# Attention rows of an output projection: split fp32 parts or native fp32 on TensorE

## The chip, the cores and the metric

The kernel runs on one core of one Trainium2 chip. The metric is the device time of one execution in microseconds (us). TensorE (PE, with its weight loads as PEld), VectorE (DVE), ScalarE (ACT), GpSimd (POOL) and SyncE (SP, which here only issues DMAs) run beside each other and meet at semaphores.

## The reference

Two layers, 256 positions (two row tiles of 128), width 1024, fp32 throughout. What matters here is the mixer and the projection that ends it:

```python
for i in range(DEPTH):
    h = h + 0.5 * _swiglu_ffn(_rms_norm(h, ffn1_norm[i]), ffn1_w_gate_up[i], ffn1_w_down[i])
    u = _rms_norm(h, mix_norm[i])
    q, k, v, ca, cg = jnp.split(u @ w_in[i], SPLITS, axis=-1)
    ...
    attn = _sliding_window_attention(q, k, v, sinks[i])
    conv = _conformer_conv(ca, cg, conv_w[i], conv_b[i], conv_ln_g[i], conv_ln_b[i])
    mixed = jnp.concatenate([_rms_norm(attn, attn_out_norm[i]),
                             _rms_norm(conv, conv_out_norm[i])], axis=-1)
    h = h + mixed @ w_out[i]
    h = h + 0.5 * _swiglu_ffn(_rms_norm(h, ffn2_norm[i]), ffn2_w_gate_up[i], ffn2_w_down[i])
    e = _rms_norm(p[i] @ w_ple[i], ple_norm[i])
    h = h + jax.nn.sigmoid(h @ w_ple_gate[i]) * e
```

`attn` and `conv` are 512 wide each, so `w_out` has 512 attention rows and 512 convolution rows.

## The kernel before

Every large product is made of reduced fp32 parts. A weight tile `raw` comes by DMA, ACT casts it to `hi` (type fp32r), DVE or POOL subtracts to get `lo`, and `triple` (line 201) makes three matmuls of it: high by high, high by low, low by high (128 rows by 128 columns held, 512 columns streamed). A few products stay in plain fp32 instead: the scores (`kT`, `qT`), probabilities times values (`pT`, `v`), and the per-layer embedding (`pinT` by `raw32`, the tile name of a unit built without an engine). The profile records each plain fp32 matmul as two weight loads and two matmuls.

Weights go through rings of tiles: 4 slots for `raw`, 10 for `hi` and 10 for `lo`, taken in program order; a new tile waits until the one ten before it is done with.

A mixer runs as follows. Convolution inputs (`c0`, `c1`, channels split in halves), keys and values, then queries are projected; DVE applies the rotary embedding (lines 786 to 789); the depthwise convolution's 31 taps run in the background, on DVE (line 565) and as ACT products that POOL adds (lines 553, 557); the result of a half is `y` (line 567). Scores of the two row blocks follow (`sm`, line 630), then values (`v0`, `v1`), and `attn_out` (line 672): the product `o` with the reciprocal denominators, times the gain on POOL into `a`, and `a` split into `a_split` (a high part by ACT, line 689, and a low part by DVE). `uwa` are the two weight units of the attention rows, 512 columns each, of four chunks; `uwc` are those of the convolution rows.

The tail follows the string `TAIL`, "a00 s0 s1 a01 t0 a10 t1 a11 b0 b1": `a<t><n>` multiplies the attention of row tile t by column half n (`out_rows`, line 718), `s` and `t` are the layer norm of the convolution (transposes of `y` and of `yn`), `b` the convolution rows. PE's order there is fixed by the program (`manual_schedule`). The other engines' order, and PE's elsewhere, come from a scheduler that plays the program through with its own costs, so leaving instructions out also reorders others.

Of the kernel before, what the change touches and what calls it, by code (L numbers as in the profile page):

```python
# [11 lines left out]
F32 = mybir.dt.float32  # L12
F32R = mybir.dt.float32r
# [6 lines left out]
P = 128  # L20
# [51 lines left out]
UWAP = (1, 3)  # L72
# [3 lines left out]
def hybrid_trunk_kernel(  # L76
# [28 lines left out]
    V, S, GP, T = nc.vector, nc.scalar, nc.gpsimd, nc.tensor  # L105
# [3 lines left out]
    wk = ctx.enter_context(tc.tile_pool(name="wk", bufs=2))  # L109
# [9 lines left out]
    def tbank():  # L119
        return pt.tile([P, 512], F32, tag="tp", name="tbank")  # L120

    def wf(name="wf"):
        return wk.tile([P, 512], F32, tag="wf", name=name, bufs=NWF)
# [7 lines left out]
    def split_lo(eng, lo, src, hi):  # L131
        return eng.tensor_tensor(out=lo, in0=src, in1=hi.bitcast(F32), op=ALU.subtract)  # L132
# [2 lines left out]
        def __init__(self, enter, first, rest):  # L135
            self.enter, self.first, self.rest = enter, first, rest

    # ---------------------------------------------------------------- weights
    pool_lo = []

    class Unit:
# [51 lines left out]
    def unit_attn_rows(w, c0, cn, eng=V):  # L193
        def half(kv):
            def part(raw, k0, ku):
                src = w[kv * G * HD:(kv + 1) * G * HD, c0:c0 + cn].rearrange("(g d) n -> d g n", d=HD)
                return raw[kv * HD:(kv + 1) * HD], src[:, k0:k0 + ku, :]
            return part
        return Unit(G, cn, [half(0), half(1)], eng)

    def triple(xh, xl, wh, wl):
        return [(xh, wh), (xh, wl), (xl, wh)]
# [15 lines left out]
    def ordered():  # L218
        return tc.manual_schedule(engines=MANUAL)

    # -------------------------------------------------------------- constants
    h = [cp.tile([P, D], F32, name=f"h{t}") for t in range(2)]

    def h_load(t):
# [20 lines left out]
    def gain(l, name):  # L245
        o, n = off[name]
        return pcol[:, o + l * n:o + (l + 1) * n]
# [21 lines left out]
        T.transpose(tb[:, 0:NPR], prow, ident[0:NPR, 0:NPR])  # L269
        V.tensor_copy(pcol[:, 16:16 + NPR], tb[:, 0:NPR])  # L270

    # -------------------------------------------------- norms and transposes
    def scratch():
        return wk.tile([P, D], BF16, tag="wf", name="scratch", bufs=NWF)

# [19 lines left out]
    def bc(g, n=P):  # L295
        return g.unsqueeze(2).to_broadcast([P, g.shape[1], n])
# [22 lines left out]
    def transposed(X, t, b, g):  # L319
        x_split(X, t, b, x_gather(X, t, b, g))  # L320

    # -------------------------------------------------------------------- ffn
    def ffn_stage(l, wgu, wdn, gname, side, early):
        X, r = [None, None], [None, None]
        H1, HT, DN, GU, acc = {}, {}, {}, {}, []
# [85 lines left out]

        return Stage(enter, first, rest)

    # ------------------------------------------------------------------- rope
    cos2 = [cp.tile([P, 16], F32, name=f"cos{t}") for t in range(2)]
    sin2 = [cp.tile([P, 16], F32, name=f"sin{t}") for t in range(2)]

# [66 lines left out]
        V.tensor_scalar(out=ms, in0=tb[:, 0:1], scalar1=1.0 / n, scalar2=None, op0=ALU.mult)  # L484
        return rms_r(ms)

    # ------------------------------------------------------------------ mixer
    def mixer_stage(l, PT, EMB):
        w = w_in[l]
        X, r, r8 = [None] * 2, [None] * 2, [None] * 2  # L490
# [27 lines left out]
    def mixer(l, w, X, r, r8, CI, CV, proj, conv_load, PT, EMB, nxt):  # L518
# [1 line left out]
        E, emb = ple(l, up, PT)  # L520
        EMB.extend(E)

        # ---- convolution inputs and depthwise convolution
        cb = gain(l, "cb")
        Y = []

# [40 lines left out]
                V.tensor_tensor(out=y, in0=acc, in1=yp, op=ALU.add)  # L567
            Y.append(y)

        # ---- q, k, v  # L570
        ukv = unit_plain(w, 0, 8, 512, 256)
        uq = unit_plain(w, 0, 8, 0, 512)
        qT = [None, None]
# [29 lines left out]
                qT[t] = wf("qT")  # L603
                S.copy(qT[t], tb)

        # ---- attention
        DEN = [None]
        AS = []
        AT, rA, PR, RX, OB = ([None] * 2 for _ in range(5))
# [62 lines left out]
        def attn_out(b):  # L672
            ob, rexp = OB[b], RX[b]
            tb = tbank()
            for gg in range(G):
                T.transpose(tb[:, gg * P:(gg + 1) * P], rexp[:, gg * P:(gg + 1) * P], ident)
            rT = wf("rT")
            S.copy(rT, tb)
            o = wf("o")
            V.tensor_tensor(out=o, in0=ob, in1=rT, op=ALU.mult)  # L680
            sq = wf("sq")
            S.activation(sq, o, AF.Square)
            a = wf("a")
            GP.tensor_tensor(out=a.rearrange("q (k m) -> q k m", k=4), in0=o.rearrange("q (k m) -> q k m", k=4),
                             in1=bc(gain(l, "attn")), op=ALU.mult)
            if b == 0:
                AS.append(wk.tile([P, 4, 512], F32R, tag="pr", name="a_split", bufs=1))
            hi, lo = AS[0][:, 2 * b, :], AS[0][:, 2 * b + 1, :]
            S.copy(hi, a)
            split_lo(V, lo, a, hi)  # L690
            AT[b] = (hi, lo)
            rA[b] = feature_r(sq, CH)

        for it in ORDER.split():
# [16 lines left out]
            elif it[0] == "o":  # L711
                attn_out(int(it[1]))

        uwa = [unit_attn_rows(w_out[l], n * 512, 512, V) for n in range(2)]
        for u in uwa:
            u.load({}, UWAP)

        def out_rows(us, F, t, rr, n, hooks=()):
            b = bank()
            terms = []  # L720
            for k in range(4):
                cs = slice(k * P, (k + 1) * P)
                terms += triple(F[0][:, cs], F[1][:, cs], us[n].hi(k), us[n].lo(k))
            mms(b, terms, hooks=hooks)
            ns = slice(n * 512, (n + 1) * 512)
            V.scalar_tensor_tensor(out=h[t][:, ns], in0=b, scalar=rr, in1=h[t][:, ns],
                                   op0=ALU.mult, op1=ALU.add)
# [60 lines left out]
        V.tensor_tensor(out=t2[:, :, 8:16], in0=q[:, :, 0:8], in1=s3[:, :, 8:16].to_broadcast([P, n, 8]), op=ALU.mult)  # L788
        V.tensor_tensor(out=q[:, :, 0:16], in0=t1, in1=t2, op=ALU.add)

    # -------------------------------------------------------------------- ple
    def bcast_row(ap, n, tag="wf", bufs=NWF):
        b = wk.tile([P, 512], F32, tag=tag, name="brow", bufs=bufs)
        GP.dma_start(b, ap[n * 512:(n + 1) * 512].partition_broadcast(P))
# [108 lines left out]

        return finish

    # ---------------------------------------------------------------- program
    def setup():
        with tc.issue_after(last_r[1].ins), tc.issue_after(pool_lo[-1].ins):
            load_gains()
# [54 lines left out]
```

## Time and profile before

| | us |
|---|---|
| median of 3 runs | 1040.07 |
| lowest, highest | 1038.52, 1041.39 |
| span of the profiled execution | 1038.1 |
| PE busy in it | 1000.2 |
| DVE busy | 665.9 |
| ACT busy | 568.6 |
| POOL busy | 180.4 |

The span is that from the first to the last instruction of one execution; no other time of that execution is shown, and the span lies 2.0 us under the median. Two stretches of the span, one in each layer, hold the mixer: from about 200 to 312 us and from about 709 to 820 us. The rest is feed-forward and gate stages, in which PE streams without a gap. A busy share over the whole span says little about the two mixers, so they are read by windows, the chain of waits and the timeline.

### The profile page before, as it was taken

Reading aid. Unit: us, or ns where it says so; the run is one execution under the profiler, and the core shown is the slowest. Engines: PE = TensorE matmul, PEld = TensorE weight load, DVE = VectorE, ACT = ScalarE, POOL = GpSimd, SP = SyncE. Lnnn points to the kernel's source line nnn. Section 1 sums busy time; section 2 is a strip of 40 time slices with the busy share of each in tenths; the row PEclk is TensorE's granted clock in tenths of the full one; section 3 lists DMA queues with packets and bytes.
Section 4 is the critical chain, followed back from the end, with each engine's and each line's share of the span. In section 5 each row is a group of like instructions: output and inputs, shape, how many; then the busy total and the mean of one; then the engine's idle time right before and its main releaser. Section 6 shows DMA issues by size and latency. Waiting matters only on the chain.

```text
span 1038.1 us, 13499 instructions
## 1 busy us (share of the span) xinstructions
PE 1000.2 (96%) x4566; PEld 808.1 (78%) x4566; DVE 665.9 (64%) x1112; ACT 568.6 (55%) x1064; POOL 180.4 (17%) x218
## 2 busy tenths in 40 slices
PE   7999999997999999999999999999979999999996
PEld 5888888884478888888888888888736888888886
DVE  6764555789978454545775555467998865455553
ACT  6554454586956354445564445456877644454442
POOL 4400000257623000000000000002856400000001
PEclk9999999998899999999999999999989999999999
DMA  8875656554046656566556565655521565565631
GB/s 267 257 223 162 205 171 209 180 147 149 1 133 194 208 169 208 173 193 202 162 168 203 168 212 171 204 173 165 165 81 41 183 203 178 187 200 165 205 100 41
DMA packets 133397, 177.24 MB, mean 171 GB/s; under 512 B 9184, under 2 KB 109872, under 8 KB 133328
## 3 DMA queue, kind: packets, MB, share of 16 engines
q1 hardware_dynamic: 132144, 174.11, 54.0%
q0 software_dynamic: 1184, 2.27, 0.8%
q8 instruction: 36, 0.59, 0.2%
q14 instruction: 33, 0.27, 0.1%
HBM read 175.29 MB, written 1.05 MB: 170 GB/s over the span
## 4 chain that ended last, share of the span: by engine, by line
PE 84%; DVE 10%; ACT 2%; issue 2%; DMA 1%; POOL 0%; SPq 0%; POOLq 0%; DVEq 0%; ACTq 0%
PE bank L210 56%; PE abank L210 24%; DVE abank L565 4%; DVE lo L132 2%; PE tbank L351 2%; DMA raw<-in_ffn_w_gate_up_dram 1%; PE tbank L305 1%; DVE sm L630 1%; ACT sm L643 1%; DVE rp L788 0%; ACT pp L553 0%; PE tbank L482 0%; DVE rp L786 0%; DVE abank L563 0%; ACT hi L167 0%
## 5 line engine op out<-in xcount | busy, mean ns | idle before, releaser
L132 DVE TENSOR_TENSOR lo<-raw,hi 128x512 fp32r<-128x512 f32 (+1 forms) x527 | 398.1, 801 | 171.5 <-ACT hi L167 164.9
L167 ACT CAST hi<-raw 128x512 fp32r<-128x512 f32 (+1 forms) x560 | 355.9, 687 | 203.7 <-PE abank L210 117.7
L210 PE MATMUL bank<-hi,xh 128*128 128x512 f32 (+1 forms) x904 | 353.4, 391 | 1.7 <-ACT hi L167 1.7
L210 PE MATMUL bank<-hi,xl 128*128 128x512 f32 (+1 forms) x904 | 348.7, 386 | 1.5 <-DVE xl L132 1.5
L210 PE MATMUL bank<-lo,xh 128*128 128x512 f32 (+1 forms) x904 | 348.8, 386 | 0.0
L210 PEld LDWEIGHTS bank<-hi,xl 128*128 128x128 f32 x904 | 170.3, 188 | 37.2 <-DVE xl L132 3.5
L210 PEld LDWEIGHTS bank<-hi,xh 128*128 128x128 f32 x904 | 170.5, 189 | 34.1 <-ACT hi L167 2.1
L210 PEld LDWEIGHTS bank<-lo,xh 128*128 128x128 f32 x904 | 170.6, 189 | 32.5 <-DVE lo L132 0.4
L210 PE MATMUL abank<-hi,hT_hi 128*128 128x512 f32 x352 | 137.7, 391 | 0.0
L210 PE MATMUL abank<-lo,hT_hi 128*128 128x512 f32 x352 | 137.5, 391 | 0.0
L210 PE MATMUL abank<-hi,hT_lo 128*128 128x512 f32 x352 | 137.4, 391 | 0.0
L342 ACT ACTIVATE sg<-bank,r 128x256 f32<-128x256 f32 x88 | 41.7, 474 | 157.1 <-PE bank L210 157.1
L344 DVE SCALAR_TENSOR_TENSOR h<-bank,r,sg 128x256 f32<-128x256 f32 x88 | 42.3, 481 | 129.4 <-ACT sg L342 129.4
L132 POOL TENSOR_TENSOR lo<-raw,hi 128x512 fp32r<-128x512 f32 x33 | 45.0, 1384 | 234.1 <-ACT hi L167 234.1
L210 PEld LDWEIGHTS abank<-hi,hT_lo 128*128 128x128 f32 x352 | 66.1, 188 | 13.5
L210 PEld LDWEIGHTS abank<-hi,hT_hi 128*128 128x128 f32 x352 | 66.1, 188 | 13.5
L210 PEld LDWEIGHTS abank<-lo,hT_hi 128*128 128x128 f32 x352 | 66.1, 188 | 13.4
L565 DVE SCALAR_TENSOR_TENSOR abank<-uT,wconv,abank 128x256 f32<-128x256 f32 x140 | 68.0, 485 | 3.4
L557 POOL TENSOR_TENSOR pp<-pp 128x512 f32<-128x512 f32 x46 | 61.3, 1332 | 50.3 <-ACT pp L553 49.0
L285 POOL TENSOR_SCALAR ms_eps<-ms 128x1 f32<-128x1 f32 x24 | 10.0, 416 | 258.4 <-ACT scratch L292 229.1
L553 ACT ACTIVATE pp<-uT,wconv 128x256 f32<-128x256 f32 x92 | 40.8, 500 | 4.5 <-POOL pp L557 4.5
L132 DVE TENSOR_TENSOR hT_lo<-tbank,hT_hi 128x512 fp32r<-128x512 f32 x44 | 30.4, 691 | 8.2 <-ACT hT_hi L353 5.9
(173 smaller groups left out, 712.2 us busy)
## 6 DMA issues: line engine op xcount, KB each, us to landing
raw<-in_ffn_w_gate_up_dram SPq DMA_DIRECT2D x352, 256.0 KB, 4.0
raw<-in_ffn_w_down_dram SPq DMA_DIRECT2D x88, 512.0 KB, 5.6
raw<-in_w_in_dram SPq DMA_DIRECT2D x32, 256.0 KB, 3.8
raw<-in_w_ple_gate_dram SPq DMA_DIRECT2D x16, 512.0 KB, 4.4
raw<-in_w_in_dram SPq DMA_DIRECT2D x12, 512.0 KB, 4.7
raw<-in_w_out_dram SPq DMA_DIRECT2D x16, 256.0 KB, 5.6
raw<-in_w_out_dram SPq DMA_DIRECT2D x8, 512.0 KB, 3.6
raw<-in_w_ple_dram SPq DMA_DIRECT2D x4, 512.0 KB, 8.2
```

The lines of the kernel that those rows point to most:

```text
L132: return eng.tensor_tensor(out=lo, in0=src, in1=hi.bitcast(F32), op=ALU.subtract)
L167: S.copy(hi[:, sl, :], raw[:, sl, :])
L210: T.matmul(dst, a, b, start=first and i == 0, stop=last and i == n - 1)
L305: T.transpose(tb[:, i * P:(i + 1) * P], h[t][:, c * P:(c + 1) * P], ident)
L342: S.activation(s, b[:, 0:FC], AF.Silu, scale=r[t])
L344: V.scalar_tensor_tensor(out=o, in0=b[:, FC:2 * FC], scalar=r[t], in1=s, op0=ALU.mult, op1=ALU.mult)
L351: T.transpose(tb[:, k * 256 + t * P:k * 256 + (t + 1) * P], H1[j, t][:, k * P:(k + 1) * P], ident)
L553: S.activation(pp[:, c, :], uT[e][:, c, k:k + 256], AF.Copy, scale=wconv[l][:, ch, k])
L557: GP.tensor_tensor(out=yp, in0=yp, in1=pp, op=ALU.add)
L565: V.scalar_tensor_tensor(out=acc[:, c, :], in0=src, scalar=ws, in1=acc[:, c, :], op0=ALU.mult, op1=ALU.add)
L630: V.tensor_tensor_reduce(out=pr[gg][:, ks], in0=sb[:, ks], in1=masks[b], scale=1.0, scalar=sinkb[l][:, hh:hh + 1], op0=ALU.add, op1=ALU.ma ...
L643: S.activation(pr[gg][:, ks], pr[gg][:, ks], AF.Exp, bias=nm[:, hh:hh + 1], accum_out=den[:, hh:hh + 1])
```

## The change

The attention rows' weight units are built without an engine: no high or low part is made, and the DMA writes straight into a slot of the `hi` ring. The transposed attention is written by POOL as plain fp32 (`attn_t`) into the slot that `a_split` had, and `out_rows` makes one plain fp32 matmul per chunk where it made three. Comment lines are left out as well, which moves later line numbers by one.

```diff
@@ attn_out
-            a = wf("a")
-            GP.tensor_tensor(out=a.rearrange("q (k m) -> q k m", k=4), in0=o.rearrange("q (k m) -> q k m", k=4),
+            if b == 0:
+                AS.append(wk.tile([P, 2, 512], F32, tag="pr", name="attn_t", bufs=1))
+            AT[b] = AS[0][:, b, :]
+            GP.tensor_tensor(out=AT[b].rearrange("q (k m) -> q k m", k=4), in0=o.rearrange("q (k m) -> q k m", k=4),
                              in1=bc(gain(l, "attn")), op=ALU.mult)
-            if b == 0:
-                AS.append(wk.tile([P, 4, 512], F32R, tag="pr", name="a_split", bufs=1))
-            hi, lo = AS[0][:, 2 * b, :], AS[0][:, 2 * b + 1, :]
-            S.copy(hi, a)
-            split_lo(V, lo, a, hi)
-            AT[b] = (hi, lo)
@@ mixer
-        uwa = [unit_attn_rows(w_out[l], n * 512, 512, V) for n in range(2)]
+        uwa = [unit_attn_rows(w_out[l], n * 512, 512, None) for n in range(2)]
         for u in uwa:
-            u.load({}, UWAP)
+            u.load()
@@ out_rows
-                terms += triple(F[0][:, cs], F[1][:, cs], us[n].hi(k), us[n].lo(k))
+                if us[n].eng is None:
+                    terms.append((F[:, cs], us[n].hi(k)))
+                else:
+                    terms += triple(F[0][:, cs], F[1][:, cs], us[n].hi(k), us[n].lo(k))
```

**DVE, layer 0, between the rotary embedding of the first and of the second query tile.** Here `lo` are the low parts of the attention rows' weights, `abank` the convolution's sum. Before:

```order
L565 SCALAR_TENSOR_TENSOR abank<-uT_102,wconv_104,abank 128x256 x2
L132 TENSOR_TENSOR lo<-raw,hi 128x512
L565 SCALAR_TENSOR_TENSOR abank<-uT_102,wconv_104,abank 128x256 x3
L132 TENSOR_TENSOR lo<-raw,hi 128x512
L565 SCALAR_TENSOR_TENSOR abank<-uT_102,wconv_104,abank 128x256
L132 TENSOR_TENSOR lo<-raw,hi 128x512
L565 SCALAR_TENSOR_TENSOR abank<-uT_102,wconv_104,abank 128x256 x3
L786 TENSOR_TENSOR rp_2261<-q,cos_94 128x128
```

After:

```order
L788 TENSOR_TENSOR q<-rp_2221,rp_2222 128x8x16
L565 SCALAR_TENSOR_TENSOR abank<-uT_102,wconv_104,abank 128x256 x11
L785 TENSOR_TENSOR rp_2261<-q,cos_94 128x128
L786 TENSOR_TENSOR rp_2262<-q,sin_96 128x8x8
L787 TENSOR_TENSOR rp_2262<-q,sin_96 128x8x8
```

Four low parts are gone (one more stands just above the piece of before); the taps stand in one row. In the same stretch ACT loses eight casts and POOL four low parts.

**DVE, layer 0, from the second rotary embedding to the first scores.** `u` is the convolution's gated input, `sm` with `m` the masked scores and their maximum. Before:

```order
L565 SCALAR_TENSOR_TENSOR abank<-uT_102,wconv_104,abank 128x256 x2
L536 SCALAR_TENSOR_TENSOR u<-bank,r,sig 128x256
L565 SCALAR_TENSOR_TENSOR abank<-uT_102,wconv_104,abank 128x256 x10
L630 ISA sm,m<-bank,mask_97,sink_106 128x128
L630 ISA m 128x1
L630 ISA sm,m<-bank,mask_97,sink_106 128x128
L630 ISA m 128x1
L536 SCALAR_TENSOR_TENSOR u<-bank,r,sig 128x256
L567 TENSOR_TENSOR y<-abank,pp 128x512
```

After:

```order
L565 SCALAR_TENSOR_TENSOR abank<-uT_102,wconv_104,abank 128x256 x4
L536 SCALAR_TENSOR_TENSOR u<-bank,r,sig 128x256
L565 SCALAR_TENSOR_TENSOR abank<-uT_102,wconv_104,abank 128x256 x7
L567 TENSOR_TENSOR y<-abank,pp 128x512
L630 ISA sm,m<-bank,mask_97,sink_106 128x128
L630 ISA m 128x1
L630 ISA sm,m<-bank,mask_97,sink_106 128x128
L630 ISA m 128x1
L536 SCALAR_TENSOR_TENSOR u<-bank,r,sig 128x256
```

The number of taps between the first query tile's rotation and the first scores stays 23; `y` of the first half moves ahead of the scores.

**PE, layer 0, where the tail begins.** `rexp` are the denominators of row block 1, `pinT` the last of the four embedding products. Before (the pattern of `hi` and `lo` goes on to twelve matmuls, then `sq` and `y` follow):

```order
L676 MATMUL tbank<-ident,rexp 128x128 x4
L210 MATMUL abank<-raw_2464,pinT 128x512
L210 MATMUL abank<-raw_2466,pinT 128x512
L210 MATMUL bank<-hi,a_split 128x512
L210 MATMUL bank<-lo,a_split 128x512
L210 MATMUL bank<-hi,a_split 128x512 x2
```

After:

```order
L676 MATMUL tbank<-ident,rexp 128x128 x4
L210 MATMUL bank<-raw_2676,attn_t 128x512 x2
L210 MATMUL bank<-raw_2679,attn_t 128x512
L210 MATMUL abank<-raw_2464,pinT 128x512
L210 MATMUL abank<-raw_2466,pinT 128x512
L210 MATMUL bank<-raw_2679,attn_t 128x512
L482 MATMUL tbank<-ones,sq 128x1 x4
L736 MATMUL tbank<-ident,y 128x128 x8
```

The first group is four plain matmuls and starts ahead of the last embedding product. Layer 1 has the same rows on PE. On SP the eight loads of the attention rows now come behind the four of the convolution rows and the two of the embedding, and each waits for a `hi` slot that PE frees.

## Rows read from the trace of the kernel before

**Rows 1.** The page: its span, and the chain's shares by engine.

```profile
span 1038.1 us, 13499 instructions
PE 84%; DVE 10%; ACT 2%; issue 2%; DMA 1%; POOL 0%; SPq 0%; POOLq 0%; DVEq 0%; ACTq 0%
```

**Rows 2.** Windows, layer 0: us; busy PE, PEld, DVE, ACT, POOL (instructions); clock; DMA.

```profile
244.00:248.00 4.00, 1.81 (x9) 1.04 (x7) 3.75 (x9) 1.70 (x4) 4.00 (x5) 1.00 0.50 141
248.00:252.00 4.00, 2.02 (x6) 1.53 (x7) 3.39 (x13) 0.36 (x1) 3.39 (x3) 0.58 0.78 249
252.00:256.00 4.00, 4.00 (x8) 1.75 (x6) 3.51 (x14) 3.95 (x8) 1.70 (x2) 0.57 0.46 134
```

**Rows 3.** Chain of waits, both layers: start us, us on the chain, what.

```profile
229.89 1.30 DVE lo L132
...
236.25 1.30 DVE lo L132
...
249.21 0.15 DVE sm L630
...
738.72 1.30 DVE lo L132
```

**Rows 4.** Groups on DVE, 226 to 250 us: busy us, mean ns | idle before.

```profile
L565 DVE SCALAR_TENSOR_TENSOR abank<-uT,wconv,abank 128x256 f32<-128x256 f32 x25 | 12.1, 485 | 0.6
L132 DVE TENSOR_TENSOR lo<-raw,hi 128x512 fp32r<-128x512 f32 x4 | 5.2, 1308 | 0.0
L788 DVE TENSOR_TENSOR rp<-q,sin 128x64 f32<-128x64 f32 x2 | 2.6, 1315 | 0.0
...
L787 DVE TENSOR_TENSOR rp<-q,sin 128x64 f32<-128x64 f32 x2 | 0.4, 211 | 0.0
```

**Rows 5.** Instructions of tile `a`, least/median/most ns: a low part with POOL idle.

```profile
L132 DVE TENSOR_TENSOR c_lo<-a,c_hi x4: 680/681/683, 296.5 to 810.8; 128x512 fp32r<-128x512 f32 x4
```

**Rows 6.** Timeline, PE, layer 0: start, us, what [idle before, released by].

```profile
242.92 0.66 PE L602 MATMUL tbank<-ident,q 128*128 128x128 f32 x4 [2.22 <-DVE q L789]
...
245.21 0.60 PE L210 MATMUL bank<-kT,qT 128*128 128x256 f32 x2
...
249.98 1.19 PE L210 MATMUL bank<-kT,qT 128*128 128x256 f32 x2 [4.17 <-DVE m L630]
```

**Rows 7.** Timeline, PE: plain fp32 matmuls, at half clock and at full.

```profile
269.91 3.18 PE L210 MATMUL abank<-raw,pinT 128*128 128x512 f32 x4
...
275.52 1.88 PE L210 MATMUL abank<-raw,pinT 128*128 128x512 f32 x4
...
277.24 1.02 PE L210 MATMUL abank<-pT,v 128*128 128x512 f32 x2
```

**Rows 8.** Chain of waits: one attention group of twelve matmuls, layer 0 and 1.

```profile
292.42 2.79 PE bank L210 x12
...
796.22 3.73 PE bank L210 x12
```

**Rows 9.** Timeline, PE: waits within the tail, layer 0 twice, layer 1.

```profile
287.71 0.65 PE L737 MATMUL tbank<-ident,y 128*128 128x128 f32 x4 [0.67 <-DVE ms L484]
...
291.79 0.63 PE L749 MATMUL tbank<-ident,yn 128*128 128x128 f32 x4 [0.65 <-DVE yn L744]
...
795.11 1.11 PE L737 MATMUL tbank<-ident,y 128*128 128x128 f32 x4 [1.47 <-DVE ms L484]
```

**Rows 10.** Timeline, layer 1: the gain on POOL, and the first attention matmul.

```profile
783.43 1.05 POOL L684 TENSOR_TENSOR a<-o,pcol 128x512 f32<-128x512 f32 x1
...
788.57 0.79 PE L210 MATMUL bank<-hi,a_split 128*128 128x512 f32 x1
```

**Rows 11.** Weight loads by tile, least/median/most ns: plain fp32, then fp32r.

```profile
L210 PEld LDWEIGHTS abank<-raw,pinT x32: 190/190/337, 269.1 to 788.1; 128*128 128x128 f32 x32
...
L210 PEld LDWEIGHTS bank<-hi,a_split x64: 187/188/337, 282.4 to 805.8; 128*128 128x128 f32 x64
```

**Rows 12.** DMA issues, the attention rows' weights: KB each, us to landing.

```profile
raw<-in_w_out_dram SPq DMA_DIRECT2D x16, 256.0 KB, 5.6
```

## Prediction

> **What bounds the kernel now.** I read the page first, then the chain of waits, then windows and timeline of the two mixers. The chain belongs to PE for 84% and to DVE for 10% [rows 1]; the reader should ask where that DVE share lies. It lies in the mixers. In layer 0 the chain runs through DVE from about 217 us to the first scores at 249.21, and the low parts of the attention rows' weights are links of it, 1.30 us at a time [rows 3]; layer 1 repeats the pattern (738.72 stands for its four). While DVE works that off, PE waits: 2.22 us for the rotated second query tile, then 4.17 us for DVE to empty a score bank [rows 6], and in that stretch its granted clock falls to 0.58 and 0.57 [rows 2], the lower of its two levels (1.2 GHz) for most of it. From about 268 us PE works nearly without a gap through the tail: only 0.67 and 0.65 us of waiting stand in layer 0's tail and 1.47 us in layer 1's [rows 9]. So the mixer has a front that DVE sets and a tail that PE sets. The change takes work from the front's engine and gives work to the tail's.
>
> **The change part by part.** *The tail's matmuls.* A plain fp32 matmul is two records. At full clock four records begin at 275.52 and the next at 277.24 [rows 7]: 1.72 / 4 = 0.43 us a record, 0.86 us a matmul, weight loads included. A group `a<t><n>` was twelve fp32r matmuls in 2.79 us [rows 8]; it becomes 4 x 0.86 = 3.44 us, so 0.65 us more, and four groups make 2.6 us a layer. Against that stand the waits. In layer 0 the 0.67 us was for a small DVE instruction standing behind four low parts and one update of `h`; now two low parts stand there. The 0.65 us for `yn` is covered by the longer group a01, which runs meanwhile. If both go, layer 0's tail costs 2.6 - 1.3 = 1.3 us. In layer 1 the wait of 1.47 us is of the first kind, and the group behind it took 3.73 us in place of 2.79, since the clock had fallen during the wait [rows 8, 9]: 2.6 - 1.5 - 0.9 = 0.2 us. If the waits stay, it is 2.6 us each. I take 1.3 and 0.2, because DVE loses the instructions that stood ahead of the awaited ones.
>
> *The front.* DVE loses four low parts of 1308 ns mean, 5.2 us [rows 4]; the taps before the first scores stay 23. A low part alone is 0.68 us [rows 5]; the rest of the 1.31 is a wait inside the instruction while POOL is working, and the same shows in the rotation, 1.32 us for one product and 0.21 for another of the same shape [rows 4]. So the saving is 4 x 0.68 = 2.7 us if that waiting moves on to the instructions behind, and 5.2 us if it goes too. Upwards PE sets the limit: its last projection and first score pair end at 245.21 + 0.60, less the 2.22 us wait [rows 6], at 243.6; the first score instruction stood at 249.21 [rows 3], so it can come 5.6 us earlier, and 0.7 us more is saved behind it, as `y` (another 128 x 512 sum, as long as the low part of [rows 5]) has moved ahead: 6.3 us. I take 5.2 a layer: the rows show the instructions as they stand in this very place, and POOL loses four low parts there too. What follows (scores, exponentials, values) is a chain of short steps on DVE, ACT and PE which starts from the first scores, so I let the shift pass whole to the tail.
>
> The Trainium skill ("SBUF — State Buffer", section on the two sides of SBUF) says that VectorE and GpSimd hold a shared port as an exclusive lock, so that a VectorE instruction with two SBUF inputs waits for all of a GpSimd one that reads SBUF. The trace agrees as far as it goes: 1.31 against 0.68 us. By that rule the second rotation falls into a gap of POOL (its adds done, the convolution rows not yet cast) and gets faster too, and the front would save the full 6.3 us in place of 5.2.
>
> *ACT and POOL.* ACT loses eight casts a layer in the front and two in `attn_out`; POOL loses four low parts. Neither engine is the chain's in the front, so they count for nothing but for what they release sooner: the second query tile's copy stood behind four casts on ACT. The split of `a` cost nothing, as PE was busy with the last embedding product meanwhile; were that cover gone, it would be a cast and a low part, some 1.3 us. In layer 1 POOL now does two more adds (about 1.3 us each) before `attn_t`. The gain ended at 784.48 and PE's first attention matmul started at 788.57 [rows 10]; that group now goes ahead of an embedding product of 1.72 us, so the slack is 4.1 - 1.7 = 2.4 us against 2.6: 0.2 us of waiting, at most 1.3. In front of that wait PE also queues the embedding product.
>
> *Loads.* The attention rows' loads move behind the convolution rows' and the embedding's on SP, and wait for slots that the query projection frees before 242.92. They take 5.6 us to land [rows 12] and are used some 35 us later: nothing. The feed-forward loads queued behind them wait for POOL's low parts as before. Without that cover PE would stand for what is left of the eight landings.
>
> *The sum.* -2 x 5.2 + 1.3 + 0.2 + 0.2 = -8.7 us. The profiled execution's span of 1038.1 would become 1029.4; the median is 2.0 us above that span, so 1040.07 - 8.7 = 1031.4 us. With the front at 6.3 it is 1029; with the tails at 2.6 each, 1035.
>
> **The rivals.** *The saving shrinks to the instruction's own length.* POOL still has eight low parts of the convolution rows to do. If they come to stand beside the rotation, DVE waits there as it did in the low parts. Front -2.7, tails +2.6, so 2 x (-2.7 + 2.6) = -0.2: 1039.9 us. For it: the 1.32 us of a rotation product. Against: those eight wait for slots that the last convolution projection frees, which lies behind the rotation.
>
> *The clock stays up.* If PE's wait of 4.17 us shrinks to 1 or 2, the clock may not fall, and the three later score pairs take 0.60 instead of 1.19 us [rows 6]. Front -6.3 - 1.5, tails as taken: 2 x -7.8 + 1.7 = -13.9: 1026.2 us.
>
> *Slower: the tail's first groups at the lower clock.* At half clock the same plain matmul took twice: 0.85 us a record at 269.91 [rows 7]. If the clock is down when a00 and a01 run, each takes 6.8 in place of 3.4 us: 6.7 us more a layer. -8.7 + 13.4 = +4.7: 1044.8 us. It decides as soon as PE stands before the tail for as long as it stood at 249.98; against it, PE was at full clock from 276 us on in layer 0, and the embedding products ahead keep it busy.
>
> *Slower: bare weight loads.* A plain fp32 load is 190 ns against 188 [rows 11]. If its loads were not hidden, 64 of them would add 12.2 us, so +3.5: 1043.6 us. The 0.43 us spacing contains its loads, which speaks against it. The Trainium skill ("TensorE: Matmul & The Clock Gate", weight-path modes) excludes fp32 from fast weight loading, which speaks against this change; the two rows show no difference that could matter.
>
> **How the numbers follow.** Forecast 58% (1029 to 1035 us, at 1031.4); shrunk saving 17% (1039.9); clock up 17% (1026.2); lower clock in the tail 5% (1044.8); bare loads 3% (1043.6). The range 1024 to 1040.5 leaves out part of the clock case's far side, part of the shrunk case and the two slow ones, about 2 in 10. About 0.3% (3.1 us) is what a measurement tells from no change: faster means under 1036.9. Forecast (0.55) and clock case (0.17) give 0.72; the shrunk case (0.16) and the forecast's edge (0.03) give 0.19 for the same; the rest, 0.09, is slower.
>
> **What would show it.** Front: the first `sm` instruction 4.5 to 6 us earlier, counted from the first query tile's rotation, and PE's wait before the third score product under 3 us. Rule of the port: rotation products of 0.2 to 0.3 us. Tail: attention groups of about 3.45 us with records 0.43 apart, no wait over 0.3 us before the transposes of `y` and `yn`. It is wrong if the records stand 0.85 apart, if the scores come early but `attn_t` does not, or if PE waits for `attn_t` by over 1 us.

## The result, and the profile after

The changed kernel takes 1029.92 us (median of 4 runs, 1027.85 to 1030.14) against 1039.3 us before in the same comparison: a ratio of 0.9899 (95% interval 0.9882 to 0.9917). Four more executions later gave 1029.76 us and 0.9907 (0.9891 to 0.9924). The prediction was 1031.4 us, with a range of 1024 to 1040.5.

The page of after, its span, busy times and the chain's shares by engine (against [rows 1]):

```profile
span 1028.4 us, 13368 instructions
PE 1000.8 (97%) x4534; PEld 799.3 (78%) x4534; DVE 648.1 (63%) x1100; ACT 560.4 (54%) x1044; POOL 168.5 (16%) x210
...
PE 92%; DVE 4%; ACT 2%; DMA 1%; POOL 1%; issue 1%; SPq 0%; POOLq 0%; DVEq 0%; ACTq 0%
```

PE is as busy as before (1000.8 against 1000.2 us), so the 9.7 us between the spans are waiting of PE that went; DVE's part of the chain fell from 10% to 4%. Where it went is seen in the front of layer 0. The chain of waits of after, start us, us on the chain, what (against [rows 3]):

```profile
239.29 1.85 PE bank L210 x8
...
241.36 1.37 PE bank L210 x6
...
242.75 0.35 DVE sm L630
```

Before, this stretch of the chain was DVE's taps and low parts. Now the chain runs through PE's projection, and DVE's first score instruction starts as PE's first score pair ends (241.36 + 1.37 = 242.73). DVE's own work ends there too (`y`, at 242.07 + 0.69 = 242.76), so the two bounds have met. The timeline of PE in after, start, us, what [idle before, released by] (against [rows 6]):

```profile
238.69 0.60 PE L602 MATMUL tbank<-ident,q 128*128 128x128 f32 x4
...
242.12 0.59 PE L210 MATMUL bank<-kT,qT 128*128 128x256 f32 x2
243.53 0.67 PE L210 MATMUL bank<-kT,qT 128*128 128x256 f32 x2 [0.81 <-DVE m L630]
...
249.62 0.33 PE L661 MATMUL tbank<-ident,sm 128*128 128x128 f32 x1 [1.93 <-ACT sm L643]
```

The wait of 2.22 us for the rotated queries is gone, the one of 4.17 us is 0.81 us, and a new one of 1.93 us has opened behind the scores, for ACT's exponentials. The clock in the windows (us; busy PE, PEld, DVE, ACT, POOL; clock; DMA) stays up where it had fallen in [rows 2], and falls a little later instead:

```profile
244.00:248.00 4.00, 3.53 (x11) 1.30 (x9) 3.74 (x16) 3.50 (x8) 4.00 (x4) 1.00 0.70 214
248.00:252.00 4.00, 2.38 (x7) 1.52 (x8) 3.74 (x15) 3.99 (x17) 2.67 (x3) 0.78 0.58 180
...
260.00:264.00 4.00, 3.71 (x9) 2.02 (x10) 3.71 (x10) 3.97 (x9) 3.07 (x3) 0.57 0.00 0
```

Groups on DVE from the first query rotation to the first scores (busy us, mean ns | idle before; against [rows 4]):

```profile
L565 DVE SCALAR_TENSOR_TENSOR abank<-uT,wconv,abank 128x256 f32<-128x256 f32 x25 | 12.2, 487 | 0.7
L787 DVE TENSOR_TENSOR rp<-q,sin 128x64 f32<-128x64 f32 x2 | 1.5, 770 | 0.0
L786 DVE TENSOR_TENSOR rp<-q,sin 128x64 f32<-128x64 f32 x2 | 1.5, 764 | 0.0
...
L567 DVE TENSOR_TENSOR y<-abank,pp 128x512 f32<-128x512 f32 x1 | 0.7, 692 | 0.1
L788 DVE TENSOR_TENSOR q<-rp,rp 128x128 f32<-128x128 f32 x2 | 0.6, 278 | 0.0
```

The four low parts (5.2 us) are gone, the taps are the same, and the rotation became shorter too: its sums (L788 now) take 278 ns, where before had (least/median/most ns):

```profile
L789 DVE TENSOR_TENSOR q<-rp,rp x2: 976/996/1015, 228.5 to 241.9; 128x128 f32<-128x128 f32 x2
```

The tail, timeline of PE in layer 0 (against [rows 7 to 9]; eight records are one group of four plain matmuls), and under it a group on the chain:

```profile
273.44 2.74 PE L210 MATMUL bank<-raw,attn_t 128*128 128x512 f32 x6
276.02 1.88 PE L210 MATMUL abank<-raw,pinT 128*128 128x512 f32 x4
277.74 1.02 PE L210 MATMUL bank<-raw,attn_t 128*128 128x512 f32 x2
...
279.41 1.07 PE L736 MATMUL tbank<-ident,y 128*128 128x128 f32 x8
...
284.67 0.63 PE L748 MATMUL tbank<-ident,yn 128*128 128x128 f32 x4 [0.76 <-DVE yn L743]
```

```profile
285.30 3.44 PE bank L210 x8
```

Six records begin at 273.44 and the next at 276.02: 0.43 us a record. A group is 3.44 us, as worked out. The wait ahead of the transposes of `y` is gone, the one for `yn` stands.

**Where the 9.2 us are.** Four marks cut each mixer: the first query rotation on DVE, the first score instruction on DVE, the start of the block of the last embedding product and the attention groups on PE, and PE's row sums ahead of the convolution rows. Starts from the timelines give these lengths in us (front, middle, tail):

| kernel | layer 0 | layer 1 |
|---|---|---|
| before | 23.30, 31.88, 17.18 | 23.31, 29.19, 18.99 |
| after | 17.34, 30.69, 19.01 | 17.35, 31.31, 19.00 |
| after, second trace | 17.34, 30.69, 19.00 | 17.34, 31.32, 19.00 |
| front_work_kept | 23.30, 30.77, 19.00 | 23.31, 29.19, 19.00 |
| half_front_work | 20.66, 30.75, 19.00 | 20.65, 29.64, 18.99 |
| no_low_parts | 18.00, 29.72, 17.12 | 17.99, 31.36, 19.04 |
| low_all_pool_b | 19.19, 30.21, 26.56 | 19.22, 30.63, 26.64 |
| yn_early | 17.34, 29.72, 18.70 | 17.34, 29.77, 18.70 |

From before to after: fronts -11.9, middles -1.2 and +2.1, tails +1.8 and 0.0, together -9.2 us. The two spans differ by 9.7 us; the other 0.5 us had been gained before the mixer of layer 0 (first query rotation at 225.41 against 225.91). The second trace of after starts its mixer at 225.89 and has a span of 1028.9 us, so that 0.5 us belongs to the execution and not to the change. The lengths are those of the traced executions; how far the middles hold for the others is taken up below.

### The profile page after: what moved, and what is told of

The parts are those of the page before. It is cut to its first block, busy times and chain, and to the rows that moved or that the text cites. A ratio compares the mean times of both kernels' runs of the same rounds, so it can differ in the third digit from the quotient of the medians.

```text
span 1028.4 us, 13368 instructions
## 1 busy us (share of the span) xinstructions
PE 1000.8 (97%) x4534; PEld 799.3 (78%) x4534; DVE 648.1 (63%) x1100; ACT 560.4 (54%) x1044; POOL 168.5 (16%) x210
## 4 chain that ended last, share of the span: by engine, by line
PE 92%; DVE 4%; ACT 2%; DMA 1%; POOL 1%; issue 1%; SPq 0%; POOLq 0%; DVEq 0%; ACTq 0%
PE bank L210 61%; PE abank L210 26%; PE tbank L351 2%; PE tbank L305 1%; DMA raw<-in_ffn_w_gate_up_dram 1%; DVE lo L132 1%; ACT sm L643 1%; DVE sm L630 1%; PE tbank L661 0%; PE tbank L482 0%; ACT hi L167 0%; POOL ms_eps L285 0%; DVE pT L665 0%; DVE xl L132 0%; DVE xg L310 0%
## 5 line engine op out<-in xcount | busy, mean ns | idle before, releaser
L132 DVE TENSOR_TENSOR lo<-raw,hi 128x512 fp32r<-128x512 f32 (+1 forms) x519 | 387.0, 791 | 175.0 <-ACT hi L167 168.5
L167 ACT CAST hi<-raw 128x512 fp32r<-128x512 f32 (+1 forms) x544 | 348.1, 689 | 209.7 <-PE abank L210 120.5
L132 POOL TENSOR_TENSOR lo<-raw,hi 128x512 fp32r<-128x512 f32 x25 | 33.1, 1347 | 239.4 <-ACT hi L167 239.4
L285 POOL TENSOR_SCALAR ms_eps<-ms 128x1 f32<-128x1 f32 x24 | 13.3, 554 | 260.2 <-ACT scratch L292 228.7
```

The costliest lines, as they stand in the source:

```text
L167: S.copy(hi[:, sl, :], raw[:, sl, :])
L285: GP.tensor_scalar(out=e, in0=ms, scalar1=EPS, scalar2=None, op0=ALU.add)
```

## The experiments

**Front and tail apart.** Theory: the gain is DVE's work in the front, the loss is the tail's. Rival: the gain comes from the loads that go straight to their slot, or from the attention's own split. The first kernel keeps the weights' casts and low parts in the front and multiplies as after:

```diff
-        uwa = [unit_attn_rows(w_out[l], n * 512, 512, None) for n in range(2)]
+        uwa = [unit_attn_rows(w_out[l], n * 512, 512, V) for n in range(2)]
-            u.load()
+            u.load({}, UWAP)
-                if us[n].eng is None:
-                    terms.append((F[:, cs], us[n].hi(k)))
+                if us is uwa:
+                    terms.append((F[:, cs], us[n].hi(k).bitcast(F32)))
```

> The weights of the attention rows are cast and their low parts subtracted as before (eight casts on ACT, four low parts on DVE, four on POOL a layer), but the tail multiplies as after, in plain fp32 on the cast weights; their low part is left out of the product. Theory (the gain is the front that DVE sets, the loss is the tail's four groups): the front is that of before, first scores about 23 us after the first query rotation and a PE wait of about 4.2 us, the tail that of after with groups of 3.44 us; the front's 2 x 6.0 us are gone and the time is 1039 to 1043 us. Rival (the gain comes from the attention's own split, or from loads that go straight to their slot): 1030 to 1034 us.

Measured: 1041.21 us, 1.0015 of before (1.0000 to 1.0031). The front is that of before to 0.01 us, the wait too:

```profile
249.94 1.19 PE L210 MATMUL bank<-kT,qT 128*128 128x256 f32 x2 [4.17 <-DVE m L630]
```

The tail is that of after, 19.00 us in both layers. So the whole gain lies in the work that was taken from the front, and without it plain fp32 is no gain. The rival falls as to the attention's split, which this kernel has not got either. It brings back the loads through `raw` together with the casts and low parts, so the loads are settled only by the next kernel.

The second kernel does the reverse: before's tail, with no low parts of the weights.

```diff
-                    lo = wp.tile([P, ku, n], F32R, tag="lo", name="lo")
+                    lo = hi if self.nolo else wp.tile([P, ku, n], F32R, tag="lo", name="lo")
@@ the same loop, behind the cast
+                    if self.nolo:
+                        continue
                     eng = GP if k0 + q in pool else self.eng
@@ uwa
+        for u in uwa:
+            u.nolo = True
```

> The kernel before without the low parts of the attention rows' weights: ACT still casts, nothing is subtracted on DVE or POOL, and the tail still makes three fp32r matmuls for each chunk, the second with the high part again; the low part is left out of the product. Theory: the front gains what after's does (first scores 6 us earlier than before), the tail stays at 2.79 us a group, so 1039.3 - 12 = 1027 us, up to 1028.5 where the 0.7 and 1.5 us waits of before's tail stay: 1.5 to 3 us under after. Rival (ACT's eight casts hold the query copy, and were a part of the gain): the front gains 3 to 4 us a layer, 1032 us or more.

Measured: 1029.14 us, 0.9890 of before (0.9862 to 0.9918). The front gains 5.3 us a layer, not 6.0: ACT still casts, and one rotation sum takes 0.99 us here. The loads still go through `raw`, so loads straight to the slot, and the casts with them, are worth 0.7 us of the front at most. The tail is before's, 17.12 and 19.04 us. The expected 1027 to 1028.5 us was missed by 0.6 us: the cheaper tail is worth only 0.8 us in the whole (1029.9 against 1029.1, a difference inside the two intervals), since its waits for DVE stay. PE's 5.2 us of dearer matmuls stand mostly where PE had waited.

**How much of the front's work counts.** Half of it put back, for one of the two weight units:

```diff
-        uwa = [unit_attn_rows(w_out[l], n * 512, 512, None) for n in range(2)]
+        uwa = [unit_attn_rows(w_out[l], n * 512, 512, V if n == 0 else None) for n in range(2)]
```

> After, with casts and low parts made as before for one of the two weight units of the attention rows (four casts on ACT, two low parts on DVE, two on POOL a layer) and multiplied in plain fp32 on the cast high part, the other unit as in after; the low part of that half of the weights is left out of the product. Theory (every low part on DVE costs its time in the front): 2 x 1.3 us less the 0.7 us by which DVE has slack in after, so first scores 19.2 to 20 us after the first query rotation and 1029.9 + 2 x 1.9 to 2 x 2.6 = 1033.7 to 1035.1 us. Rival 1 (the waits inside the instructions, not their number, made the cost, and with half of POOL's work they go): first scores under 18.6 us, under 1032.5 us. Rival 2 (the cost is that of any work at this place, by an order that turns for the worse): first scores at 22 us or more, 1038 us or more.

Measured: 1035.49 us, 0.9961 (0.9946 to 0.9976). First scores 20.66 us after the first rotation: over the theory's 20 and well under rival 2's 22, as the time lies 0.4 us over the theory's. The first two low parts cost 3.3 us of front, the other two 2.6, and the times 1029.8, 1035.5, 1041.2 stand 5.7 us apart. In layer 0 the two low parts take 2.1 us from the start of their rows on DVE to the start of the next, and the two rotations 5.7 us in place of 4.15: the theory had the low parts, and not what the rotation loses with them. No threshold lies between. PE's wait before the third score product is back at once, with 4.13 us.

**The same work on POOL.** If only DVE's own instructions counted, the kernel before could move them to POOL and keep its cheaper matmuls:

```diff
-UWAP = (1, 3)
+UWAP = (0, 1, 2, 3)
```

> The kernel before with all eight low parts of the attention rows' weights on POOL, none on DVE; nothing is left out. Theory A (only DVE's own work counts): the front gains as in after, the tail stays in fp32r: 1027 to 1029 us. Theory B (an instruction of DVE with two SBUF inputs waits while POOL works, so that work moved to POOL comes back as waiting): rotation products of 1.3 us and more of them, the front gains 2.7 us a layer or less: 1034 us or more. Theory C (POOL becomes late): PE waits for low parts or the layer norm waits for POOL's adds by over 1 us in the tail: 1033 to 1040 us.

> The kernel before with all eight low parts of the attention rows' weights on POOL, for a trace: its time was 1048.5 us, 9 us over before. Theory B (waits inside DVE instructions beside POOL): taps and rotation products of DVE take longer than before in the front, and the first scores come no earlier. Theory C (POOL late): the front gains 5 us or more, and PE loses 14 us or more in waits for something that POOL makes (sums of the convolution, the gain of the attention, the reciprocal roots).

Measured: 1048.8 us, 1.0084 of before (1.0059 to 1.0108), 1048.86 us in the execution with a trace. A falls. C names what cost the time, PE's waits in the tail, though the front gains less than its 5 us and the time is longer than it said. Of B only the mechanism holds, in the rotation and not in the taps: the first scores come 4.1 us earlier, where B had 2.7 us at most in its first form and none in its second. Groups on DVE in the front (busy us, mean ns | idle):

```profile
L565 DVE SCALAR_TENSOR_TENSOR abank<-uT,wconv,abank 128x256 f32<-128x256 f32 x25 | 12.2, 487 | 0.7
L788 DVE TENSOR_TENSOR rp<-q,sin 128x64 f32<-128x64 f32 x2 | 2.7, 1328 | 0.0
L789 DVE TENSOR_TENSOR q<-rp,rp 128x128 f32<-128x128 f32 x2 | 2.0, 1010 | 0.0
```

The taps, which read one operand from PSUM, do not mind POOL: 487 ns, as in after. The rotation, which reads both from SBUF, does: its sums take 1010 ns where after has 278, and the two rotations of layer 0 together 6.9 us, where before has 6.6 and after 4.15. So the front gains 4.1 us, not 6.0. And POOL, busy with low parts, is late with its sums of the convolution, in both layers; PE's timeline in layer 0:

```profile
289.63 1.54 PE L737 MATMUL tbank<-ident,y 128*128 128x128 f32 x6 [7.17 <-DVE y L567]
```

In layer 1 the wait is 8.45 us. What is saved on DVE in the front is lost twice over in the tail.

**The convolution rows in plain fp32 too.**

```diff
-        uwc = [unit_plain(w_out[l], 4, 4, n * 512, 512, V) for n in range(2)]
+        uwc = [unit_plain(w_out[l], 4, 4, n * 512, 512, None) for n in range(2)]
@@ ln_act
-            hi, lo = wr("c_hi"), wr("c_lo")
-            S.copy(hi, a)
-            split_lo(V, lo, a, hi)
-            CT[t] = (hi, lo)
+            CT[t] = a
```

> After, with the four convolution row groups of the tail in plain fp32 as well: no casts on ACT, no low parts on POOL (eight a layer) and no split of the normalized convolution; nothing is left out. Theory (plain fp32 pays only where it takes work from an engine that the path waits for; POOL's eight low parts are beside the path): PE gets 4 x 0.65 us more a layer and nothing comes back, 1029.9 + 5.2 = 1035 us, down to 1033 us where the instructions that wait beside POOL after the scores (1.2 us for one small subtraction in layer 1) get shorter. Rival (POOL's low parts hold DVE's small instructions between scores and values by more than that): 1030.5 us or less.

Measured: 1037.17 us, 0.9982 of before (0.9973 to 0.9992): 7.3 us over after, the theory's sign and more than its size. DVE's small subtraction behind the scores did get short, 0.16 us for 1.31, since POOL has nothing to do there now. It bought nothing: PE's wait of 1.93 us for the exponentials is the same in both, and the next small sum of its kind (`den`) stretched in its place, 1.06 us in the median for 0.61. The groups add 1.4 us for each row tile (the row sums of the two stand 7.76 us apart, 6.36 in after), and behind them the next stage starts late:

```profile
310.30 0.50 PE L210 MATMUL bank<-hi,xh 128*128 128x512 f32 x1 [0.54 <-ACT xh L316]
```

That is 2 x 1.4 + 0.5 = 3.3 of the 3.7 us a layer; the rest was not traced down.

**The wait for `yn`.** The prediction had it covered; it stands at 0.76 us. The chain of after in layer 1 shows what ends last there:

```profile
783.93 0.77 POOL ms_eps L285
...
785.34 0.55 POOL ms L819
...
786.27 0.57 POOL rr L287
...
787.22 0.57 POOL r L287
...
787.81 0.82 DVE yn L743
```

It is POOL's row of small instructions: the reciprocal roots of the attention and of the embedding (`ms`, `rr`) ahead of the layer norm's `r`. In layer 0, where before had this wait too, the row takes 3.8 us from its first start to its end and took 3.1, because two of its instructions grew. The timeline of POOL before; then of POOL and of DVE in after:

```profile
287.74 0.22 POOL L285 TENSOR_SCALAR ms_eps<-ms 128x1 f32<-128x1 f32 x1 [1.97 <-DVE ms L484]
288.58 0.32 POOL L820 TENSOR_TENSOR ms<-ms 128x1 f32<-128x1 f32 x1
```

```profile
279.84 0.76 POOL L285 TENSOR_SCALAR ms_eps<-ms 128x1 f32<-128x1 f32 x1 [2.47 <-DVE ms L484]
281.20 0.57 POOL L819 TENSOR_TENSOR ms<-ms 128x1 f32<-128x1 f32 x1
...
279.83 0.69 DVE L132 TENSOR_TENSOR lo<-raw,hi 128x512 fp32r<-128x512 f32 x1
281.05 0.68 DVE L132 TENSOR_TENSOR lo<-raw,hi 128x512 fp32r<-128x512 f32 x1
```

Each of the two now stands beside a low part on DVE and ends within 0.1 us of it. DVE's low parts seem to hold POOL up here as POOL held DVE up in the front; no run tests this by itself. Two edits try it: another order on PE, and the embedding's three instructions moved behind.

```diff
-TAIL = "a00 s0 s1 a01 t0 a10 t1 a11 b0 b1"
+TAIL = "a00 s0 s1 a01 a10 t0 t1 a11 b0 b1"
```

> After, with the second attention group of row tile 1 pulled ahead of the yn transposes (a00 s0 s1 a01 a10 t0 t1 a11 b0 b1). Theory (PE's wait of 0.76 us for yn is on the path in both layers and is covered by 3.44 us of matmuls): 1029.9 - 1.5 = 1028.4 us, no PE wait over 0.2 us in the tail. Rival (the wait moves on: the convolution's split for b0 now has 3.9 us instead of 7.8 us of cover): a new wait before b0 or b1 of 0.5 us or more, 1029.5 to 1031 us.

Measured: 1032.29 us, 0.9932 (0.9908 to 0.9956), 2.4 us over after: the rival's mechanism, and 1.3 us more than it said. The wait for `yn` is gone and a longer one stands before the convolution rows; the clock, 1.00 in the window of that wait, is 0.57 in the next, so that it costs more than its length. The traced execution is the longest of the four (1035.04 us, the others 1031.9 to 1032.5), so the others may have lost less by the clock:

```profile
294.19 0.50 PE L210 MATMUL bank<-hi,c_hi 128*128 128x512 f32 x1 [1.16 <-ACT c_hi L758]
```

```profile
296.00:300.00 4.00, 4.00 (x12) 3.11 (x11) 1.69 (x3) 0.21 (x1) 0.00 (x0) 0.57 0.74 245
```

The other edit:

```diff
             if n == 1:
-                ms = small(1, "ms")
-                GP.tensor_tensor(out=ms, in0=ms2[t][:, 0:1], in1=ms2[t][:, 1:2], op=ALU.add)
-                rr[t] = rms_r(ms, "rr")
+                def norm():
+                    ms = small(1, "ms")
+                    GP.tensor_tensor(out=ms, in0=ms2[t][:, 0:1], in1=ms2[t][:, 1:2], op=ALU.add)
+                    rr[t] = rms_r(ms, "rr")
+                if t == 0:
+                    norm()
+                else:
+                    LATE.append(norm)
@@ mixer, tail
+                    if it == "s1":
+                        with tc.issue_after(last_r[-1].ins):
+                            LATE.pop()()
```

> After, with three small POOL instructions of the embedding's norm (its sum, and the two of its reciprocal root, 1.4 us together, row tile 1) put behind the layer norm's own on POOL; PE's order is that of after. Theory (the wait of 0.76 us for yn in both layers is POOL's queue of small instructions, as the chain shows it): yn comes 1.4 us earlier, the wait goes, 1029.9 - 1.5 = 1028.4 us. Rival (something else is late at once: the layer norm's statistics on DVE behind low parts): a wait for yn of 0.3 us or more stays, 1029.3 us or more.

> The kernel of yn_early again, for more executions beside the kernel before. If its gain over after is real (1.2 us by the medians, 0.6 us by the waits for yn, 0.76 to 0.45 us in each layer): median 1028.2 to 1029.2 us, ratio to before 0.989 to 0.990. If it is the spread of executions: 1029.5 us or more. The wait for yn should be 0.45 us again in both layers.

Measured: 1028.71 us, 0.9899 (0.9884 to 0.9914), and 1028.56 us, 0.9896 (0.9883 to 0.9910), in five more executions. The wait falls from 0.76 to 0.45 us in both layers, where DVE's statistics behind low parts are late at once, as the rival said:

```profile
283.73 0.63 PE L749 MATMUL tbank<-ident,yn 128*128 128x128 f32 x4 [0.45 <-DVE yn L744]
```

The medians say 1.2 us less than after, the tails 2 x 0.3 us; the intervals of the two kernels overlap almost wholly. Both traced executions are the shortest of their sets (1027.39 and 1027.17 us), and in the first of them 2.5 us of what it is shorter than after lie in the two middles, not in the tail. It is the fastest kernel measured here, by a margin that these runs do not prove.

**The middle.** Its clock falls differently from kernel to kernel. The embedding product moved into the 1.93 us wait:

```diff
-ORDER = "c0 k q c1 u s0 s1 x v0 v1 p0 o0 p1 p2 o1 p3"
+ORDER = "c0 k q c1 u s0 s1 x p0 v0 v1 o0 p1 p2 o1 p3"
```

> After, with the first of the four embedding products (two plain fp32 matmuls, 1.72 us) issued on PE ahead of the values of row block 0, where PE waits 1.93 us for the exponentials. Theory A (the idle stretch between the scores and the values costs its idle time and, by the clock that falls behind it, up to 2.3 us more, so that this stage differs from one execution to the next): the wait falls below 0.5 us, the stretch behind it (values, embedding) runs at full clock in both layers, 1.7 to 4 us less a layer: 1022 to 1026.5 us. Theory B (that stage is set by the chain of maxima, exponentials and transposes, and the embedding product only moves the waiting to where it stood before): the time stays within 1 us of after, 1029 to 1031 us, with a new wait of about 1.7 us before the second values or the attention groups.

> Both of the two edits above (embedding product early, the embedding's norm behind the layer norm's on POOL). If both theories hold the two gains add up, 1020.5 to 1025 us; if only that of the POOL queue holds, 1028 to 1029.5 us.

Measured: 1029.76 us, 0.9913 (0.9898 to 0.9928), and 1028.98 us, 0.9916 (0.9888 to 0.9944), with the other edit on top. Theory B. The wait for the exponentials is 0.51 us and in emb_early's trace the mean clock rose from 0.992 to 0.996, but PE now waits later, for a bank that DVE's `o` gives free (1.64 us in layer 0, 2.2 in layer 1):

```profile
271.51 1.98 PE L210 MATMUL abank<-raw,pinT 128*128 128x512 f32 x4 [1.64 <-DVE o L680]
```

The middles of that trace are 30.93 and 29.79 us, against 30.69 and 31.31 in after. So an earlier product mostly moves PE's waiting to a later place, for maxima, exponentials and copies on DVE and ACT. What the clock takes of this stage was not separated from it.

> The changed kernel unaltered, for more executions and a second trace. Theory (between the first scores and the first attention group PE's clock falls differently from one execution to the next; front and tail do not vary): front and tail within 0.2 us of the first trace of after (first scores 17.3 us after the first query rotation, 19.0 us from the first attention group to the convolution rows), the stretch between them 29 to 31.5 us and not the same in both layers; median 1028.5 to 1030.5 us. Rival (that stretch too is fixed by the order, 30.7 us in layer 0 and 31.3 in layer 1): both within 0.2 us of these.

Measured: 1029.76 us. Front, middle and tail repeat to 0.02 us in both layers, as the rival said. That the order of the work fixes the clock is not shown by it: both traces are of executions with a mean clock of 0.992, and of the eight executions of after one, without a trace, had 0.996 and was 2 us shorter. And tail_order, whose work up to there is that of after, does not repeat the middle of layer 0 (31.11 us). On PE, DVE, ACT and POOL the instructions of the mixer up to the exponentials are the same and agree in length to 0.03 us, and then the clock falls in after and stays up in tail_order; timelines of PE, after and then tail_order:

```profile
249.78 1.44 PE L210 MATMUL bank<-kT,qT 128*128 128x512 f32 x2
...
249.97 1.03 PE L210 MATMUL bank<-kT,qT 128*128 128x512 f32 x2
```

What decides it stays open.

## Why the prediction came out right, and where its steps did not

**The front (predicted -5.2 us a layer; measured -6.0).** The mechanism is right, the term was too small. Counted from the start of each row of DVE to the start of the next, between the first rotation and the first scores of layer 0, the low parts took 4.9 us before, and the two rotations 6.6 us before and 4.15 after; `y`, which now stands ahead of the scores, takes 0.7 back, and the 24 taps read 0.75 longer by this count: -4.9 - 2.45 + 0.7 + 0.75 = -5.9. The step that failed is the choice of 5.2: it counted the waiting inside the low parts and not that inside the rotation, which the prediction had named and set aside. The limit of 6.3 us held 5.6 for the first scores and 0.7 behind them; the scores passed their 5.6, since PE's first score pair ended 17.3 us after the first rotation and not at the 17.7 that the prediction worked out. The signs for it came as written: first scores 4.5 to 6 us earlier (6.0), a wait before the third score product under 3 us (0.81). The second rotation of after, DVE, and POOL beside it:

```profile
233.81 0.29 DVE L785 TENSOR_TENSOR rp<-q,cos 128x128 f32<-128x128 f32 x1
234.01 1.32 DVE L786 TENSOR_TENSOR rp<-q,sin 128x64 f32<-128x64 f32 x1
235.25 0.21 DVE L787 TENSOR_TENSOR rp<-q,sin 128x64 f32<-128x64 f32 x1
...
235.78 0.28 DVE L788 TENSOR_TENSOR q<-rp,rp 128x128 f32<-128x128 f32 x1
```

```profile
233.94 1.30 POOL L557 TENSOR_TENSOR pp<-pp 128x512 f32<-128x512 f32 x1 [0.42 <-ACT pp L553]
238.22 9.95 POOL L132 TENSOR_TENSOR lo<-raw,hi 128x512 fp32r<-128x512 f32 x8 [2.98 <-ACT hi L167]
```

One product meets POOL's add and takes 1.32 us; the one ahead of the add and the two rotation instructions behind it fall into POOL's gaps and take 0.2 to 0.3. That is what the Trainium skill ("SBUF — State Buffer", section on the two sides of SBUF) says of the port that VectorE and GpSimd share: an exclusive lock, held for the whole instruction. The sign written for that rule, rotation products of 0.2 to 0.3 us, came in part, with the 1.32 us against it; the time by that rule (first scores 5.6 us earlier) was nearer than the forecast's 5.2.

**The tail (predicted +1.3 and +0.2, with 0.2 for `attn_t`; measured +1.8 and 0.0).** The price of a plain group is exact, 3.44 us, but one wait was misjudged. The wait behind DVE's `ms` went in both layers. The one for `yn` did not: the step said that the longer group a01 covers it, but POOL's row ahead of `yn` got longer by about as much (3.8 us for 3.1, as shown above), and the wait is 0.76 us for 0.65. So layer 0 is 2.6 - 0.67 + 0.11 = 2.0, of which the trace shows 1.8: behind a transpose the old groups stood 2.87 us from start to start, so that a plain one costs 0.56 to 0.58 us there and not 0.65. Layer 1 had no wait for `yn` before and has 0.76 us now. From start to start its groups cost 1.3 us, with the lower clock that the second had before; its waits are 0.9 us less, and transposes and row sums 0.4 less, together 0.0. Nothing waited for `attn_t`: in layer 1 POOL had it at 775.8, 1.7 us ahead of PE's first matmul on it at 777.54, where the prediction had worked out that POOL is 0.2 us late.

**The clock (predicted: nothing outside the tail; measured -1.2 and +2.1).** This is the step that was missing. The prediction let the shift of the scores pass whole to the tail. In layer 1 the pair of values and the first embedding product ran at full clock before and at the lower of its two levels after; the timeline of before, then of after:

```profile
776.51 1.02 PE L210 MATMUL abank<-pT,v 128*128 128x512 f32 x2
777.37 1.88 PE L210 MATMUL abank<-raw,pinT 128*128 128x512 f32 x4
```

```profile
764.51 1.92 PE L210 MATMUL abank<-pT,v 128*128 128x512 f32 x2
766.22 3.31 PE L210 MATMUL abank<-raw,pinT 128*128 128x512 f32 x4
```

That is 0.85 + 1.4 = 2.3 us; the granted clock was 1.00 from 776 to 780 us before and is 0.50 from 764 to 768 after. In layer 0 it went the other way: the first embedding product takes 2.1 us from start to start, where before had 3.0. Ahead of it PE worked in pieces with waits between them, in both kernels; why it falls at 764 in one and not at 776 in the other was not settled. Both traces of yn_early, whose PE order is that of after, have the first embedding product of either layer at full clock (1.88 us) and middles of 29.7 to 29.8 us. So the two terms hold for the traced executions, and how much of them is in the medians stays open.

**The rivals.** The clock case has its first half (the score pairs take 0.6 us, the wait shrank; they are five pairs, not three) and not its time, since the clock falls further on. The shrunk saving did not come. The low_all_pool kernels put POOL beside the rotation, as it asks; the rotation keeps its length there, and the front still gains 4.1 us. The lower clock in a00 and a01 did not come. Bare weight loads did not come either: 64 loads of 190 ns lie inside the 0.43 us of a record.

```profile
L210 PEld LDWEIGHTS bank<-raw,attn_t x64: 190/190/192, 273.3 to 795.7; 128*128 128x128 f32 x64
```

**The sum.** -10.4 + 1.7 = -8.7 us was predicted, -11.9 + 1.8 + 0.9 = -9.2 us measured. The front was 1.5 us too small and the clock's 0.9 us was not in it; the closeness is in part two errors that cancel, which is luck. Of the 1.5 us between 1031.4 and 1029.92, half is the base: the prediction started from 1040.07, and the kernel before took 1039.3 in the comparison.

## What to carry to other kernels

Dearer matmuls on the busiest engine can pay, where what they replace stands on the path of another engine and the matmuls themselves stand where their engine waits: the same edit was worth 9 us on the attention rows and cost 7 us on the convolution rows. Read the stretch, not the kernel's shares, and price an instruction of DVE with two SBUF operands together with what POOL does beside it, its neighbours too. A wait that is removed by an order comes back at the next thing that is late, so ask for that before counting it.

## What the runs showed of the hardware

- A plain fp32 matmul of 128 x 128 by 512 took 0.86 us at full clock, against 0.23 us for one in fp32r (2.79 / 12): about 3.7 to one, and so 1.23 of the three that it replaces.
- DVE instructions stretched beside POOL by the kind of their operands: two from SBUF, from 0.28 to 1.01 us for a rotation sum; one from PSUM, 485 to 487 ns in the four fronts read for this, however busy POOL was.
- The middles, with their low stretches of the granted clock, repeated between two traces of after (30.69 and 31.31 us, then 30.69 and 31.32) and between two of yn_early (29.7 to 29.8 in all four). But tail_order, which does the same work as after up to there, had 31.11 us in layer 0: the same instructions got another clock.
- POOL's instructions on 128 x 1 elements took 0.76 and 0.57 us beside a low part on DVE, where the same ones took 0.22 and 0.32 in the kernel before.
